# Rotary scores over 128 rows in a hybrid decoder trunk, and last projection weights loaded last

## The chip, the core and the metric

The kernel runs on one core of a Trainium2 chip. The time is the device time of one execution in microseconds (us). The core has five engines that run their own instruction queues in order: TensorE (PE, matrix products into PSUM), VectorE (DVE), ScalarE (ACT), GpSimd (POOL) and SyncE (SP, which issues the loads here).

## What is computed

Two post-norm decoder layers on 256 tokens of width 1024, each a token mixer and a gated feed-forward block. Layer 0 mixes with latent attention, which the change touches:

```python
proj = h @ w_in                                   # 1024 -> 256 + 256 + 64
c_q  = rms_norm(proj[..., :256], q_norm)
c_kv = rms_norm(proj[..., 256:512], kv_norm)
k_rope = apply_rope(proj[..., 512:], cos, sin)    # one key of 64 for all heads
q = (c_q @ w_uq)                                  # 8 heads, 128 plain + 64 rotary
q = concat(q[..., :128], apply_rope(q[..., 128:], cos, sin))
k = concat(k_plain, k_rope);  o = causal_softmax_attention(q, k, v, 192 ** -0.5)

def apply_rope(x, cos, sin):
    x1, x2 = halves(x)
    return concat(x1 * cos - x2 * sin, x2 * cos + x1 * sin)
```

Ahead of it stands `h = x * (1 + scale(c)) + shift(c)`, where scale and shift are products of a vector `c` with 1024x6144 modulation weights.

## The kernel before

Activations lie transposed: 128 features on the partitions, 256 tokens on the columns, eight such pieces `j` for the width of 1024.

The first stage (loads from line 413 on, loop from line 573 to 607) goes over `j`. For each `j` a 1 MB piece `early[j]` of modulation weights is loaded; `mod_half` multiplies each of its two halves on DVE with the spread vector and sums them into a column (`modc`); one small addition gives `gb0`; ACT makes `hin[:, j]`; PE adds five products to the accumulators of the latent query (`cqp`), the latent key (`ckp`) and the rotary key (`krp`). The projection weights come as `iraw[k]`, two `j` in each, and POOL copies their 64 rotary columns twice side by side into `krw`, so that `krp` holds the rotary key on rows 0 to 63 and again on rows 64 to 127. All loads but one are issued by SP in the order written; the positions (`posi`) are issued by ACT, and the parameters `par_sb` second of all. `rotary()` is a generator in five steps that makes the tables `sin_t` and `cos_t`: the first step runs ahead of the loop, the others at the ends of the first `j`.

The second stage (lines 1032 to 1107) makes queries, keys and values. `low_rank` is eight products of 256 columns on PE into one of three PSUM buffers (`mm`). For the rotary parts, `rope_mul` takes a result of 128 rows (two heads of 64) and makes two products on DVE, with `cos_t` and with `sin_t`; `rope_add` adds them on PE, one through the identity and one through a matrix `swap` that exchanges half blocks of 32 rows, and ACT copies the sum out. That is done once for the key (`kr`, 256 columns) and twice for the queries (`qr`, 512 columns, four heads each). Between stand the chains `rk` (scale of the latent key) and `rq` (scale of the query).

The third stage goes over the heads (class `Head`). `scores` is, for each head, a product of 128 rows (`q`, `kk`) and a product of 64 rows (`qr`, `kr`) into the same accumulator; then come softmax (DVE, ACT), `turn`, `weigh` and `rest`, and the projection in pieces. Heads 0 and 1 are scored ahead of the values (`vps`), the others in a loop.

DVE has other work throughout: modulation halves of later blocks (`mods`) and the low parts of weights that are split in two (`fill`, after ACT's `split_hi`). When the program is written, a model of the engines' times (`Clock`) places such work where it expects DVE or ACT to stand idle by 0.45 us or more; `settled` and `need` force it ahead of its readers. The order is then fixed.

Of the kernel before, what the change touches and what calls it, by code (L numbers as in the profile page):

```python
# [12 lines left out]
F32 = mybir.dt.float32  # L13
# [4 lines left out]
ALU = mybir.AluOpType  # L18
PSUM = bass.MemoryType.PSUM

P = 128
D = 1024
S = 256
NJ = D // P
H = 8
# [27 lines left out]
OFF_ROT = OFF_KN + 2  # L53
OFF_POS = OFF_ROT + 2
NPAR = OFF_POS + 2

# [132 lines left out]
def trunk_kernel(ctx: ExitStack, tc: tile.TileContext, xT, c_col, pos_row, par, mod,  # L189
# [5 lines left out]
    G = nc.gpsimd  # L195
# [3 lines left out]
    HALF = 1024  # L199
# [4 lines left out]
    one = ring("one", 1)  # L204
    raws = ring("raws", RAWS)
    wts = ring("wts", PIECES)
    act = ring("act", 2)
# [21 lines left out]
    def mod_half(u, raw, n):  # L229
        li, p0, j0, p1, j1 = units[u]  # L230
        pp, jj = ((p0, j0), (p1, j1))[n]
        w = raw[:, n * D:(n + 1) * D]
        V.scalar_tensor_tensor(w, w, 1.0, cbf, op0=ALU.mult, op1=ALU.mult,
                               accum_out=modc[:, li, pp, jj:jj + 1])
# [175 lines left out]
    par_sb = one.tile([P, NPAR], F32, name="par_sb")  # L410
    cst_sb = par_sb[:, OFF_ROT:OFF_ROT + 2]
    posci = par_sb[:, OFF_POS:OFF_POS + 2].bitcast(I32)
    z = one.tile([P, NJ, S], F32, name="z")
    Q.dma_start(cc, c_col)
    A.dma_start(posi, pos_row.to_broadcast([P, S]))
    Q.dma_start(par_sb, par)
    ce = one.tile([P, NJ], F32, name="ce")
# [3 lines left out]
    def load_mod(j, *parts):  # L421
        if j not in early:
            ring, tag = (wts, "wx") if j < PIECES else (raws, "raw")
            early[j] = ring.tile([P, 2 * HALF], F32, name="early", tag=tag)
        for p in parts:
            Q.dma_start(early[j][:, p * HALF:(p + 1) * HALF], mod[j][:, p])
        if not parts:
            Q.dma_start(early[j], mod[j])

    def load_in(k):  # L430
        iraw[k] = raws.tile([P, 2, 576], F32, name="iraw", tag="raw")
        Q.dma_start(iraw[k], w_mla_in[k])

    def load_x(a, b):
        Q.dma_start(z[:, a:b], xT[:, a:b])

    load_mod(0, 0)
    load_x(0, 2)
    load_mod(0, 1)
    load_in(0)  # L440
    load_mod(1)
# [8 lines left out]
    load_mod(6)  # L450
    load_in(3)
    load_mod(7, 0, 1)

# [48 lines left out]
    G.memset(meanr, 1.0 / 256)  # L502
    swap = one.tile([P, P], F32, name="swap")
    iv = ident.rearrange("p (a b c) -> p a b c", a=2, b=2)
    sv = swap.rearrange("p (a b c) -> p a b c", a=2, b=2)
    for b in range(2):
        G.tensor_copy(sv[:, :, b], iv[:, :, 1 - b])

# [26 lines left out]
    def rotary():  # L535

        ang = tmp.tile([P, S], F32, name="ang", tag="g")
        V.tensor_copy(posb, posi)
        V.tensor_scalar(ang, posb, cst_sb[:, 0:1], None, op0=ALU.mult)
        for dst, turn, quarter in ((sin_t, 0.0, 0.0), (cos_t, 0.25, math.pi / 2)):  # L540
            n = tmp.tile([P, S], F32, name="n", tag="t")
            V.tensor_scalar(n, ang, INV_2PI, turn, op0=ALU.mult, op1=ALU.add)
            V.tensor_scalar(n, n, MAGIC, None, op0=ALU.add)
            V.tensor_scalar(n, n, MAGIC, None, op0=ALU.subtract)
            yield
            V.scalar_tensor_tensor(dst, n, -PI2_A, ang, op0=ALU.mult, op1=ALU.add)
            V.scalar_tensor_tensor(dst, n, -PI2_B, dst, op0=ALU.mult, op1=ALU.add)
            V.scalar_tensor_tensor(dst, n, -PI2_C, dst, op0=ALU.mult, op1=ALU.add)
            if quarter:
                V.tensor_scalar(dst, dst, quarter, None, op0=ALU.add)  # L550
            V.tensor_scalar(dst, dst, PI_SAFE, -PI_SAFE, op0=ALU.min, op1=ALU.max)
            A.activation(dst, dst, AF.Sin)
            yield
        A.mul(sin_t, sin_t, cst_sb[:, 1:2])
        table(AF.Abs_reciprocal_sqrt, cos_t)
        yield

    angles = rotary()
    next(angles)
    V.tensor_copy(cb[:, 4:8], cps[1])  # L560
# [4 lines left out]
    wuqn = act.tile([P, 2, D], F32, name="wuqn", tag="v", bufs=1)  # L565
    lat = act.tile([P, 4, S], F32, name="lat", tag="hl")
    wuk = act.tile([P, 2, D], F32, name="wuk", tag="hh")
# [5 lines left out]
    for j in range(NJ):  # L573
        k = j % 2
        raw = iraw[j // 2]
        if k == 0:
            krw = tmp.tile([P, 2, 2, 64], F32, name="krw", tag="krw", bufs=1)
            G.tensor_copy(krw, raw[:, :, 512:576].unsqueeze(2).to_broadcast([P, 2, 2, 64]))
        for n in range(2):
            mod_half(j, early[j], n)  # L580
        (wts if j < PIECES else raws).done.add(early[j][:].tensor.name)
# [14 lines left out]
        for i in range(5):  # L596
            ps = cqp[:, i] if i < 2 else (ckp[:, i - 2] if i < 4 else krp)
            w = raw[:, k, i * P:(i + 1) * P] if i < 4 else krw[:, k].rearrange("p a b -> p (a b)")
            T.matmul(ps, w, hin[:, j], start=(j == 0 and i in (0, 2, 4)), stop=(j == NJ - 1 and i in (1, 3, 4)))
# [441 lines left out]

    def rope_mul(src, space):
        n = src.shape[1]
        m = space.rearrange("p (a n) s -> p a n s", a=2)
        V.tensor_mul(m[:, 0], src, cos_t.unsqueeze(1).to_broadcast([P, n, S]))
        V.tensor_mul(m[:, 1], src, sin_t.unsqueeze(1).to_broadcast([P, n, S]))
        return m

    def rope_add(dst, m):
        n = dst.shape[1]  # L1050
        ps = psy.tile([P, n, S], F32, name="swp", tag="y")
        T.matmul(ps, ident, m[:, 0], start=True, stop=False)
        T.matmul(ps, swap, m[:, 1], start=False, stop=True)
        A.copy(dst, ps)

    q = act.tile([P, H, S], F32, name="q", tag="q", bufs=1)
    qr = act.tile([P, 4, S], F32, name="qr", tag="qr", bufs=1)
    kr = one.tile([P, 1, S], F32, name="kr")
    rk = tmp.tile([P, S], F32, name="rk", tag="rstd", bufs=1)
# [10 lines left out]
    for i in range(2):  # L1070
        A.activation(sqq[i], cqp[:, i], AF.Square)
    mk = rope_mul(krp.unsqueeze(1), z[:, 0:2])
    ps0 = low_rank(wuqr, 0, 0)
    for i in range(2):
        T.matmul(rkp, meanr, sqk[i], start=(i == 0), stop=(i == 1))
    m0 = rope_mul(ps0, hin[:, 0:4])
    rsqrt(rk, rkp, eps_rms)
    for i in range(2):
        V.scalar_tensor_tensor(lat[:, 2 + i], ckp[:, i], kn2[:, i:i + 1], rk, op0=ALU.mult, op1=ALU.mult)
    ps1 = low_rank(wuqr, 0, 2)  # L1080
    rope_add(kr, mk)
    for i in range(2):
# [5 lines left out]
    V.tensor_scalar(rq, rq, -0.5 * MLA_SCALE, None, op0=ALU.mult)  # L1088
    A.copy(q[:, 0:2], low_rank(wuqn, 0, 0))
    rope_add(qr[:, 0:2], m0)  # L1090
    m1 = rope_mul(ps1, hin[:, 4:8])
    A.copy(q[:, 2:4], low_rank(wuqn, 0, 2))
    rope_add(qr[:, 2:4], m1)
    for h in range(4, H, 2):
        A.copy(q[:, h:h + 2], low_rank(wuqn, 0, h))
# [7 lines left out]
    for h in range(H):  # L1103
        po = (h % 2) * 64
        heads.append(Head(h, [(q[:, h], kk[:, h]), (qr[po:po + 64, h // 2], kr[po:po + 64, 0])],
                          v[:, :, h * P:(h + 1) * P], oh, ol))
# [266 lines left out]
```

## Time and profile before

| | us |
|---|---|
| median of 3 runs | 618.01 (617.64 to 618.23) |
| profiled execution | 617.5 |
| its span in the profile | 615.7 |
| PE busy | 590.1 (96%) |
| DVE busy | 484.5 (79%) |
| ACT busy | 365.0 (59%) |

Times in the rows are counted from the span's start. A busy PE is not PE at its peak, since ends of pipelined products are modelled. Idle time of an engine that doesn't set the end costs nothing. In a timeline, "x4" merges four instructions of one form that follow each other; the pitch from one to the next is shorter than the length of one, because starts overlap ends.

### The profile page before, as it was taken

Reading aid. Unit: us, or ns where it says so; the run is one execution under the profiler, and the core shown is the slowest. Engines: PE = TensorE matmul, PEld = TensorE weight load, DVE = VectorE, ACT = ScalarE, POOL = GpSimd, SP = SyncE. Lnnn points to the kernel's source line nnn. Section 1 sums busy time; section 2 is a strip of 40 time slices with the busy share of each in tenths; the row PEclk is TensorE's granted clock in tenths of the full one; section 3 lists DMA queues with packets and bytes.
Section 4 is the critical chain, followed back from the end, with each engine's and each line's share of the span. In section 5 each row is a group of like instructions: output and inputs, shape, how many; then the busy total and the mean of one; then the engine's idle time right before and its main releaser. Section 6 shows DMA issues by size and latency. Waiting matters only on the chain.

```text
span 615.7 us, 11313 instructions
## 1 busy us (share of the span) xinstructions
PE 590.1 (96%) x4572; PEld 563.3 (91%) x4572; DVE 484.5 (79%) x937; ACT 365.0 (59%) x660; POOL 11.5 (2%) x27
## 2 busy tenths in 40 slices
PE   3799999999999999999999999999999999999994
PEld 2577579999999999999999999999999999999992
DVE  6866989899968889889788888388997765656545
ACT  3345686777754355555778776777685545454423
POOL 2000000100000000000010000000000000000000
PEclk9999999999999999999999999999999999999998
DMA  8999868447868888889237979424789655552001
GB/s 307 417 421 421 307 226 312 176 163 278 310 233 303 298 316 309 307 311 370 102 137 274 342 283 365 175 69 147 271 314 321 246 168 181 200 193 82 2 1 69
DMA packets 22372, 149.68 MB, mean 243 GB/s; under 512 B 2608, under 2 KB 3120, under 8 KB 5040
## 3 DMA queue, kind: packets, MB, share of 16 engines
q1 hardware_dynamic: 22176, 148.83, 66.3%
q8 instruction: 36, 0.59, 0.4%
q10 hardware_dynamic: 144, 0.13, 0.1%
q14 instruction: 16, 0.13, 0.1%
HBM read 147.90 MB, written 1.05 MB: 242 GB/s over the span
## 4 chain that ended last, share of the span: by engine, by line
PE 57%; issue 31%; DMA 5%; DVE 3%; ACT 2%; POOL 1%; POOLq 0%; SPq 0%; ACTq 0%; DVEq 0%
PE abps L171 19%; PE pps L171 10%; PE ffy L171 9%; PE wops L171 7%; DMA early<-in_mod_dram 5%; PE lrp L171 3%; PE fps L171 2%; PE sps L171 2%; DVE z L171 1%; PE po L171 1%; PE vps L171 1%; ACT z L171 1%; POOL st L745 1%; PE swp L171 1%; PE tps L171 1%
## 5 line engine op out<-in xcount | busy, mean ns | idle before, releaser
L171 PE MATMUL abps<-nh,wx 128*128 128x256 f32 x1344 | 233.0, 280 | 0.0
L171 DVE TENSOR_TENSOR wx<-raw,wx 128x1024 fp32r<-128x1024 f32 x166 | 198.7, 1218 | 17.4 <-ACT wx L171 17.3
L171 PEld LDWEIGHTS abps<-nh,wx 128*128 128x128 f32 x1344 | 201.7, 188 | 0.1
L171 ACT CAST wx<-raw 128x1024 fp32r<-128x1024 f32 x166 | 170.7, 1045 | 38.2 <-PE ffy L171 18.0
L171 PE MATMUL abps<-nl,wx 128*128 128x256 f32 x672 | 179.8, 279 | 0.0
L171 PE MATMUL ffy<-gh,wx 128*128 128x256 f32 x704 | 126.0, 280 | 0.0
L171 PEld LDWEIGHTS abps<-nl,wx 128*128 128x128 f32 x672 | 123.0, 188 | 0.0
L171 PEld LDWEIGHTS ffy<-gh,wx 128*128 128x128 f32 x704 | 107.8, 188 | 0.0
L171 PE MATMUL ffy<-gl,wx 128*128 128x256 f32 x352 | 98.7, 280 | 0.0
L171 DVE SCALAR_TENSOR_TENSOR raw<-raw,cb 128x1024 f32<-128x1024 f32 x80 | 96.3, 1217 | 0.1
L171 DVE SCALAR_TENSOR_TENSOR t<-abps,par_sb,t 128x255 f32<-128x255 f32 x84 | 40.4, 481 | 41.7 <-ACT t L171 40.2
L171 ACT ACTIVATE t<-abps,par_sb 128x256 f32<-128x256 f32 x42 | 23.6, 561 | 73.9 <-PE abps L171 73.8
L171 PEld LDWEIGHTS ffy<-gl,wx 128*128 128x128 f32 x352 | 66.1, 188 | 0.0
L171 PE MATMUL wops<-oh,wx 128*128 128x256 f32 x256 | 46.3, 283 | 0.0
L171 PE MATMUL pps<-nh,wx 128*128 128x256 f32 x224 | 40.3, 285 | 0.0
L171 PEld LDWEIGHTS wops<-oh,wx 128*128 128x128 f32 x256 | 39.2, 189 | 0.1
L171 PE MATMUL wops<-ol,wx 128*128 128x256 f32 x128 | 36.0, 281 | 0.2 <-DVE ol L171 0.2
L171 PEld LDWEIGHTS pps<-nh,wx 128*128 128x128 f32 x224 | 34.0, 188 | 0.3
L171 ACT ACTIVATE z<-z,st 128x128 f32<-128x128 f32 x64 | 27.0, 449 | 10.1 <-DVE st L171 9.9
L171 PE MATMUL pps<-nl,wx 128*128 128x256 f32 x112 | 30.1, 280 | 0.0
L171 ACT ACTIVATE t<-t 128x256 f32<-128x256 f32 x44 | 18.3, 416 | 16.6 <-DVE t L171 15.4
L171 DVE TENSOR_TENSOR g<-t,abps 128x256 f32<-128x256 f32 x42 | 17.5, 417 | 13.5 <-ACT t L171 13.4
(183 smaller groups left out, 692.2 us busy)
## 6 DMA issues: line engine op xcount, KB each, us to landing
raw<-in_w_f_dram SPq DMA_DIRECT2D x66, 1024.0 KB, 5.1
raw<-in_mod_dram SPq DMA_DIRECT2D x40, 1024.0 KB, 6.5
raw<-in_w_qk_dram SPq DMA_DIRECT2D x8, 1024.0 KB, 5.9
early<-in_mod_dram SPq DMA_DIRECT2D x6, 1024.0 KB, 13.9
raw<-in_w_mla_o_dram SPq DMA_DIRECT2D x4, 1024.0 KB, 7.7
raw<-in_w_v_dram SPq DMA_DIRECT2D x4, 1024.0 KB, 7.5
raw<-in_w_moba_o_dram SPq DMA_DIRECT2D x4, 1024.0 KB, 6.7
iraw<-in_w_mla_in_dram SPq DMA_DIRECT2D x4, 576.0 KB, 13.5
```

The costliest lines, as they stand in the source:

```text
L171: b = f(*args, **kw)
L745: G.tensor_tensor(st[:, 4:6], st[:, 2:4], mhalf, op=ALU.pow)
```

## The change

The scores' rotary part is taken over 128 rows. A query's rows 0 to 63 hold its product with the cosines and rows 64 to 127 its product with the sines (`rope_q`: four products on DVE, each over 64 partitions and 512 columns, from PSUM straight to `qr`). The key's rows 0 to 63 hold the turned key and rows 64 to 127 its quarter turn, so that the product over 128 rows gives the same score. The key is made by two products over 64 partitions and one product on PE with a matrix `turn`, which POOL builds. The turns of the queries on PE, their copies on ACT and the factor of sign on `sin_t` go away. Half of `qr` lies in a longer `lat`.

In the first stage, `posi` moves to SP's queue behind the first `x`, `par_sb` goes behind the first modulation half, the last `iraw` is loaded in halves with its second half behind all modulation weights, the last modulation half is loaded and multiplied in two quarters, `krw` is copied for each `j`, and all steps of `rotary` run in the loop.

```diff
-    A.dma_start(posi, pos_row.to_broadcast([P, S]))
-    Q.dma_start(par_sb, par)
...
     load_mod(0, 0)
+    Q.dma_start(par_sb, par)
     load_x(0, 2)
     load_mod(0, 1)
+    Q.dma_start(posi, pos_row.to_broadcast([P, S]))
     load_in(0)
...
-    load_in(3)
-    load_mod(7, 0, 1)
+    load_in(3, 0)
+    load_mod(7, 0, 2, 3)
+    load_in(3, 1)
...
-    for b in range(2):
-        G.tensor_copy(sv[:, :, b], iv[:, :, 1 - b])
+    turn = one.tile([P, P], F32, name="turn")
+    for b, sign in enumerate((-1.0, 1.0, 1.0, -1.0)):
+        G.tensor_scalar(turn[:, 32 * b:32 * b + 32], ident[:, 96 - 32 * b:128 - 32 * b], sign, None, op0=ALU.mult)
+    G.tensor_tensor(turn, turn, ident, op=ALU.add)
...
-        A.mul(sin_t, sin_t, cst_sb[:, 1:2])
...
-    next(angles)
...
-    lat = act.tile([P, 4, S], F32, name="lat", tag="hl")
+    lat = act.tile([P, NJ, S], F32, name="lat", tag="hl")
...
-        if k == 0:
-            krw = tmp.tile([P, 2, 2, 64], F32, name="krw", tag="krw", bufs=1)
-            G.tensor_copy(krw, raw[:, :, 512:576].unsqueeze(2).to_broadcast([P, 2, 2, 64]))
+        krw = tmp.tile([P, 2, 64], F32, name="krw", tag="krw")
+        G.tensor_copy(krw, raw[:, k, 512:576].unsqueeze(1).to_broadcast([P, 2, 64]))
         for n in range(2):
-            mod_half(j, early[j], n)
+            if (j, n) == (NJ - 1, 1):
+                part = tmp.tile([P, 2], F32, name="part", tag="part", bufs=1)
+                for i in range(2):
+                    w = early[j][:, (2 + i) * HALF // 2:(3 + i) * HALF // 2]
+                    V.scalar_tensor_tensor(w, w, 1.0, cbf[:, i * HALF // 2:(i + 1) * HALF // 2], op0=ALU.mult,
+                                           op1=ALU.mult, accum_out=part[:, i:i + 1])
+                V.tensor_add(modc[:, 0, 0, j:j + 1], part[:, 0:1], part[:, 1:2])
+            else:
+                mod_half(j, early[j], n)
...
-    def rope_mul(src, space):
...
-    def rope_add(dst, m):
...
+    def rope_q(dst, ps):
+        dst = dst.rearrange("p (b a) s -> p b a s", a=2)
+        for a in range(2):
+            i = slice(64 * a, 64 * a + 64)
+            for o, t_ in ((0, cos_t), (64, sin_t)):
+                V.tensor_mul(dst[o:o + 64, :, a], ps[i], t_[i].unsqueeze(1).to_broadcast([64, 2, S]))
...
-    mk = rope_mul(krp.unsqueeze(1), z[:, 0:2])
+    for o, t_ in ((0, cos_t), (64, sin_t)):
+        V.tensor_mul(z[o:o + 64, 0], krp[o:o + 64], t_[o:o + 64])
     ps0 = low_rank(wuqr, 0, 0)
...
-    m0 = rope_mul(ps0, hin[:, 0:4])
+    rope_q(qr[0], ps0)
     rsqrt(rk, rkp, eps_rms)
...
     ps1 = low_rank(wuqr, 0, 2)
-    rope_add(kr, mk)
+    krt = psy.tile([P, S], F32, name="krt", tag="y")
+    T.matmul(krt, turn, z[:, 0], start=True, stop=True)
+    A.copy(kr, krt)
...
-    A.copy(q[:, 0:2], low_rank(wuqn, 0, 0))
-    rope_add(qr[:, 0:2], m0)
-    m1 = rope_mul(ps1, hin[:, 4:8])
-    A.copy(q[:, 2:4], low_rank(wuqn, 0, 2))
-    rope_add(qr[:, 2:4], m1)
-    for h in range(4, H, 2):
+    rope_q(qr[1], ps1)
+    for h in range(0, H, 2):
         A.copy(q[:, h:h + 2], low_rank(wuqn, 0, h))
...
-        heads.append(Head(h, [(q[:, h], kk[:, h]), (qr[po:po + 64, h // 2], kr[po:po + 64, 0])],
+        heads.append(Head(h, [(q[:, h], kk[:, h]), (qr[h // 4][:, h % 4], kr)],
```

## Rows read from the trace of the kernel before

**Rows 1.** the page: span; each engine's busy time, share of it, instructions
```profile
span 615.7 us, 11313 instructions
PE 590.1 (96%) x4572; PEld 563.3 (91%) x4572; DVE 484.5 (79%) x937; ACT 365.0 (59%) x660; POOL 11.5 (2%) x27
```

**Rows 2.** by stretch: length, busy time of PE, PEld, DVE, ACT, POOL; clock; DMA
```profile
8.35:26.04 17.69, 11.40 (x38) 8.81 (x39) 17.27 (x46) 7.30 (x13) 1.22 (x2) 1.00 1.02 421
...
39.20:62.52 23.32, 23.32 (x105) 19.13 (x104) 15.94 (x30) 10.74 (x20) 0.00 (x0) 1.00 0.98 407
39.20:102.98 63.78, 63.54 (x339) 49.27 (x338) 52.47 (x128) 40.50 (x98) 0.00 (x0) 1.00 0.87 337
89.40:102.98 13.58, 13.58 (x109) 13.37 (x110) 12.64 (x27) 9.25 (x19) 0.00 (x0) 1.00 0.91 338
```

**Rows 3.** waits of TensorE from 39.2 us on: total, times, longest
```profile
PE bc L171 <- POOL st L745: 1.5, 4, 0.7
```

**Rows 4.** timeline of the first stage: start, length, engine, operation, idle before it
```profile
1.63 0.42 SPq L171 DMA_DIRECT2D early<-in_mod_dram  x1
5.35 0.28 DVE L171 CAST posb<-posi 128x256 f32<-128x256 int32 x1
6.39 0.62 DVE L171 TENSOR_SCALAR n<-n 128x256 f32<-128x256 f32 x2
28.26 1.22 DVE L171 SCALAR_TENSOR_TENSOR early<-early,cb 128x1024 f32<-128x1024 f32 x1 [2.22 <-DMA early<-in_mod_dram]
29.41 1.22 DVE L171 SCALAR_TENSOR_TENSOR early<-early,cb 128x1024 f32<-128x1024 f32 x1
36.29 0.60 ACT L171 ACTIVATE hin<-z,gb 128x256 f32<-128x256 f32 x1 [2.00 <-DVE gb L171]
```

**Rows 5.** timeline of TensorE (PE) from 43 to 56 us
```profile
43.52 0.59 PE L171 MATMUL swp<-z,ident 128*128 128x256 f32 x2
43.95 0.59 PE L171 MATMUL swp<-z,swap 128*128 128x256 f32 x2
47.00 1.02 PE L171 MATMUL swp<-hin,ident 128*128 128x512 f32 x2
48.72 1.89 PE L171 MATMUL lrp<-lat,wuqn 128*128 128x256 f32 x8
55.62 7.07 PE L171 MATMUL lrp<-lat,wuk 128*128 128x256 f32 x32
```

**Rows 6.** timeline of VectorE (DVE) from 41 to 47 us
```profile
41.13 0.69 DVE L171 TENSOR_TENSOR hin<-lrp,cos_t 128x512 f32<-128x512 f32 x1 [0.91 <-PE lrp L171]
41.74 0.68 DVE L171 TENSOR_TENSOR hin<-lrp,sin_t 128x512 f32<-128x512 f32 x1
44.00 0.88 DVE L171 SCALAR_TENSOR_TENSOR lat<-ckp,kn,rk 128x256 f32<-128x256 f32 x2
45.93 0.21 DVE L171 SCALAR_TENSOR_TENSOR y<-rqp,eps_rms,y 128x2 f32<-128x2 f32 x1
46.65 0.68 DVE L171 TENSOR_TENSOR hin<-lrp,cos_t 128x512 f32<-128x512 f32 x1
```

**Rows 7.** timeline of TensorE and its weight loads (PEld), first scores
```profile
62.52 0.82 PE L171 MATMUL sps<-kk,q 128*128 128x128 f32 x4
65.82 7.13 PE L171 MATMUL vps<-wuv,lat 128*128 128x512 f32 x16
63.27 0.52 PEld L171 LDWEIGHTS sps<-kr,qr 64*128 64x128 f32 x4 [0.33 <-issue]
```

**Rows 8.** the chain that ended last, in order of time, heads 4 and 5
```profile
79.66 0.26 DVE z L171
82.64 0.26 DVE z L171
```

**Rows 9.** waits of VectorE from 39.2 to 118 us
```profile
DVE wx L171 <- ACT wx L171: 5.7, 2, 5.2
DVE z L171 <- PE wops L171: 0.8, 1, 0.8
```

More of the change, by code (lines that the diff above doesn't have):

```diff
@@ L53 @@
 OFF_ROT = OFF_KN + 2
-OFF_POS = OFF_ROT + 2
+OFF_POS = OFF_ROT + 1
 NPAR = OFF_POS + 2
@@ L410, in trunk_kernel @@
     par_sb = one.tile([P, NPAR], F32, name="par_sb")
-    cst_sb = par_sb[:, OFF_ROT:OFF_ROT + 2]
+    cst_sb = par_sb[:, OFF_ROT:OFF_ROT + 1]
     posci = par_sb[:, OFF_POS:OFF_POS + 2].bitcast(I32)
@@ L425, in load_mod, with load_in @@
         for p in parts:
-            Q.dma_start(early[j][:, p * HALF:(p + 1) * HALF], mod[j][:, p])
+            a, b = ((0, HALF), (HALF, 2 * HALF), (HALF, 3 * HALF // 2), (3 * HALF // 2, 2 * HALF))[p]
+            Q.dma_start(early[j][:, a:b], mod[j].rearrange("p a n -> p (a n)")[:, a:b])
         if not parts:
             Q.dma_start(early[j], mod[j])
-    def load_in(k):
-        iraw[k] = raws.tile([P, 2, 576], F32, name="iraw", tag="raw")
-        Q.dma_start(iraw[k], w_mla_in[k])
+    def load_in(k, *parts):
+        if k not in iraw:
+            iraw[k] = raws.tile([P, 2, 576], F32, name="iraw", tag="raw")
+        for p in parts:
+            Q.dma_start(iraw[k][:, p], w_mla_in[k][:, p])
+        if not parts:
+            Q.dma_start(iraw[k], w_mla_in[k])
     def load_x(a, b):
@@ L502, in trunk_kernel @@
     G.memset(meanr, 1.0 / 256)
-    swap = one.tile([P, P], F32, name="swap")
-    iv = ident.rearrange("p (a b c) -> p a b c", a=2, b=2)
-    sv = swap.rearrange("p (a b c) -> p a b c", a=2, b=2)
-    for b in range(2):
-        G.tensor_copy(sv[:, :, b], iv[:, :, 1 - b])
+    turn = one.tile([P, P], F32, name="turn")
+    for b, sign in enumerate((-1.0, 1.0, 1.0, -1.0)):
+        G.tensor_scalar(turn[:, 32 * b:32 * b + 32], ident[:, 96 - 32 * b:128 - 32 * b], sign, None, op0=ALU.mult)
+    G.tensor_tensor(turn, turn, ident, op=ALU.add)
     mask = one.tile([P, 384], F32, name="mask")
@@ L597, in trunk_kernel @@
             ps = cqp[:, i] if i < 2 else (ckp[:, i - 2] if i < 4 else krp)
-            w = raw[:, k, i * P:(i + 1) * P] if i < 4 else krw[:, k].rearrange("p a b -> p (a b)")
+            w = raw[:, k, i * P:(i + 1) * P] if i < 4 else krw.rearrange("p a b -> p (a b)")
             T.matmul(ps, w, hin[:, j], start=(j == 0 and i in (0, 2, 4)), stop=(j == NJ - 1 and i in (1, 3, 4)))
@@ L1040, in low_rank @@
         return ps
-    def rope_mul(src, space):
[L1043 to L1047, printed above, removed]
-    def rope_add(dst, m):
[L1050 to L1054, printed above, removed]
+    def rope_q(dst, ps):
[4 more added lines that the diff above has]
+                V.tensor_mul(dst[o:o + 64, :, a], ps[i], t_[i].unsqueeze(1).to_broadcast([64, 2, S]))
     q = act.tile([P, H, S], F32, name="q", tag="q", bufs=1)
-    qr = act.tile([P, 4, S], F32, name="qr", tag="qr", bufs=1)
-    kr = one.tile([P, 1, S], F32, name="kr")
+    qr = lat[:, 4:8], act.tile([P, 4, S], F32, name="qr", tag="qr", bufs=1)
+    kr = one.tile([P, S], F32, name="kr")
     rk = tmp.tile([P, S], F32, name="rk", tag="rstd", bufs=1)
@@ L1103, in trunk_kernel @@
     for h in range(H):
-        po = (h % 2) * 64
-        heads.append(Head(h, [(q[:, h], kk[:, h]), (qr[po:po + 64, h // 2], kr[po:po + 64, 0])],
+        heads.append(Head(h, [(q[:, h], kk[:, h]), (qr[h // 4][:, h % 4], kr)],
                           v[:, :, h * P:(h + 1) * P], oh, ol))
@@ L1315 @@
     freq = (ROPE_BASE ** (-np.arange(32) / 32)).astype(np.float32)
-    cst = np.stack([np.tile(freq, 4), np.tile(np.repeat(np.array([1.0, -1.0], np.float32), 32), 2)], axis=1)
+    cst = np.tile(freq, 4).reshape(P, 1)
     pos = np.ascontiguousarray(a["positions"].astype(np.int32).reshape(1, S))
```

## The prediction

> **What bounds the kernel now.** I read the page first: TensorE (PE) is busy for 590.1 of 615.7 us [rows 1], so time can only come from PE's work, or from the stretch in which it starves. The list of PE's waits places that stretch: after 39.2 us the largest entry is 1.5 us in four pieces [rows 3]. All other starving is ahead of 39.2 us. The timeline of that first stage shows what ends there: VectorE (DVE) multiplies each 1 MB piece of modulation weights as it lands. It runs almost unbroken to 26.04 us (17.27 of 17.69 us busy [rows 2]), waits 2.22 us for the sixth piece, and from 28.26 us goes from half to half until the last `hin` starts at 36.29 us [rows 4]. Then I read the stretch that is rewritten. From 39.2 to 62.5 us PE is busy throughout [rows 2], so work taken off PE there moves the first scores. One stretch is another matter: from about 74.5 to 89.4 us the chain runs through DVE and ScalarE, and a head's softmax follows the last at a distance of 2.98 us (79.66 to 82.64 [rows 8]), whatever PE does. From 89.4 us PE leads again. So what is won ahead of 74.5 us is kept to the end, if DVE can follow; what PE saves inside the head loop is worth nothing.
>
> **Part 1, loads and the angles.** The first modulation half is issued one place earlier, 0.47 us at most (it stood at 1.63 us, a slot of 0.42 us and a gap [rows 4]). Bytes are the same. The first stage of `rotary` (four operations from 5.35 to 7.01 us [rows 4]), which stood in idle time ahead of the loop, enters DVE's unbroken run, and each later stage moves one `j` back. DVE therefore reaches the sixth piece about 1.65 us later; the 2.22 us of idle time there [rows 4] covers it, and 0.57 us of cover is left. Without that cover it would cost 1.65 us. The last projection half now lands behind the last modulation piece, so that piece lands some 0.7 us earlier (295 KB at the 421 GB/s of [rows 2]). But DVE is the limit by then: from 28.26 to 36.29 us it runs six halves at 1.15 us (28.26 to 29.41 [rows 4]), 6.9 of the 8.0 us; the rest is small additions and some 0.3 us of waits. Those go. The last half is cut in two quarters: neither row shows a quarter, so the pair lies between 1.15 us (no fixed part) and 2.3 us (nothing saved); near the lower end, for the same form on 256 columns takes 0.44 us of 0.88 for two [rows 6], so 1.22 us, plus one small addition of 0.16. That eats what the 0.3 gave. What is left is the earlier stream: **-0.25 us**, between -0.8 (whole slot, and quarters that hide) and +0.6 (the cover too short after a later `posi`). The eight smaller copies of `krw` and the five operations that build `turn` go to GpSimd, which is busy for 11.5 us in all [rows 1]; the last copy, after the late half, has some 3 us until the last `krp`. SyncE's queue gets three more issues of 0.42 us and is ahead of the landings: nothing.
>
> **Part 2, the turns leave PE.** Of the key's two products one stays: -0.43 us (43.52 to 43.95 [rows 5]). Each of the two query turns was four passes, 47.00 to 48.72 us [rows 5]: -1.72 us each. Together **-3.87 us** of PE, all in its unbroken stretch; ScalarE loses two copies of 0.59 us that were not on the path. DVE pays: four products over 64 partitions for two over 128, twice. The trace has none over 64 partitions. Its ends are half price (0.34 us) and full price, 0.61 us from one 128x512 row to the next (41.13 to 41.74 [rows 6]); I take full price, since in this trace a vector operation's time goes with its columns. The Trainium skill (VectorE: DVE Perf Modes, the section on why `tensor_reduce` can't reduce along the partition axis) says that each of the 128 partition lanes is an independent pipeline, which speaks against this part: half the lanes idle and nothing is saved. By the page the sum below stands as it is; no row here shows it.
>
> Full price gives +1.22 us for each of the two sets. The first set ends at 43.65 instead of 42.43 us. The `rk` chain behind it ended at 44.88 and now ends near 45.95; its reader on PE, `wuk`, starts near 52, so nothing waits. Behind it come the four small `rq` operations (0.72 us, 45.93 to 46.65 [rows 6]) and then the second set, 46.65 to 49.17 us. **Here is a new wait.** The second `wuqr` result sits in one of three PSUM buffers, and the third pair of `wuqn` products needs that buffer. PE gets there at 48.30 us (first pair 0.43 earlier, then 1.73 us for each pair), so it stands until about 49.2: +0.9 us. Queued behind it are the other `wuqn` and `wuk` products and the first scores, so it counts in full. Bounds: 0 at half price, 2.05 if the planner puts a modulation half of 1.15 us ahead of the second set. Net of part 2: **-2.95 us**, between -3.87 and -1.8.
>
> **Part 3, scores over 128 rows.** A weight load ahead of or behind a 64-row group of scores starts 0.33 us after the one before it [rows 7], eight times at the 64-row groups, and the first two heads' four groups take 3.30 us, 62.52 to 65.82 [rows 7]. A 128-row group has 384 columns twice; by the pitch of 0.43 us for 256 columns twice [rows 5] that is 0.65 us, four of them 2.6 us: -0.7. The third head's pair saves 0.3 more. The other five are inside the loop of 2.98 us [rows 8] and give nothing. **-1.0 us**, between 0 (the gaps have another cause) and -1.3. The Trainium skill (TensorEngine Tiling (Array Packing), Tiling Modes, Key Properties) says that changing the tiling mode drains the array; by that the gaps go away, and the sum is this one. The same page (Overview, Theoretical Speedup) offers up to 2x for a contraction of 64 or less, which the change gives up; the kernel before doesn't take it, its 64-row groups run one after another.
>
> **Part 4, DVE's queue.** The same queue holds the modulation halves and the splits of weights, and PE needs them at the first projection. From 39.2 to 102.98 us DVE is busy for 52.5 of 63.8 us [rows 2]: 11.3 idle. The change takes 2.45 us of it for products and 3.95 us by moving PE forward, 6.4 in all. Most idle time there is latency that can't be filled; 5.7 us of it is a wait for ScalarE's half of a split [rows 9], and I take that as usable, since landed modulation pieces can be run in it. That leaves +0.7 us, which the 0.8 us of waiting for the projection at 102 us [rows 9] would absorb only if the planner's order allows. **+0.7 us**, between 0 and +4.9 (none of the 5.7 usable, the 0.8 and another 0.7 absorbed).
>
> **The sum.** -0.25 - 2.95 - 1.0 + 0.7 = -3.5 us. Against the profiled execution's 617.5 us (span 615.7): 614.0. The median of the runs is 618.0, 0.5 above it, so **614.5 us**.
>
> **Rivals.** (a) Everything is kept: no buffer wait, no backlog, the slot at the start: -0.8 - 3.87 - 1.0 = -5.7, near 612.3. For it: half-price products would do it, and the idle 5.7 us is large enough almost alone. Against: three estimates must all fall well. (b) The new wait comes at its worst (2.05) and the backlog at about 2: -0.25 - 1.8 - 1.0 + 2 = near -1, 617. For it: DVE is busy for 12.64 of the last 13.58 us before the projection [rows 2]. (c) Slower: DVE's backlog becomes the bound at the first normalisation. The planner sets the order from its own durations, and before it left 5.2 us idle at one place [rows 9], so it misjudges by that much. If the 5.7 us stays idle again and one more modulation piece (2.3 us) must be run just ahead of the column sums, the price is 4.9 + 2.3 = 7.2 against a gain of 4.2: 621. It decides from a lateness of 5.7 us at 103 us (4.2 + 1.5 of slack). Against: splits for the next block stand in the same stretch and can be put off. (d) The 128-row scores aren't shorter: 615.5, inside my range. That the change doesn't do what it says: the turned key would still need its two products; the code has one.
>
> **How the numbers follow.** A measurement of this kernel tells about 0.2% (1.2 us) from no change: faster is below 616.8. My forecast with its neighbours from 613.2 to 615.9 us, (d) in it: 0.50. (a) with what lies below 613.2: 0.21. Between 615.9 and 616.8: 0.08. (b), within 0.2%: 0.12. (c): 0.09. So faster 0.79, same 0.12, slower 0.09. Range: it leaves out (c) and the far ends of (a) and (b): 611.9 to 617.3.
>
> **What would show it.** Right: the last `hin` at 36.0 us, first `wuk` product near 52.4, first scores near 59.3, third pair of `wuqn` behind a gap of about 0.9 us, no gaps of 0.33 us in the scores, products over 64 partitions at 0.61 us. The lead should be about 4.2 us at the third head's softmax and 3.5 us in the first block. Wrong: DVE late at the projection, waits of PE on a split or on `z` between 85 and 120 us, or a lead that grows in the head loop.

## The result, and the profile after

The changed kernel is slower. Its median of 4 runs is 624.45 us (623.66 to 625.32) against 617.83 us for the kernel before, measured beside it: a ratio of 1.0107, 95% interval 1.0091 to 1.0123. The forecast was 614.5. The profiled span grows by 7.1 us, and TensorE (PE) does less than before in it (586.6 us busy for 590.1, [rows 1]):

```profile
span 622.8 us, 11309 instructions
PE 586.6 (94%) x4562; PEld 565.1 (91%) x4562; DVE 488.6 (78%) x944; ACT 362.7 (58%) x657; POOL 16.0 (3%) x34
```

So PE waits more than before. Its list of waits from 39.2 to 125 us (total, times, longest) names the place; before, nothing over 1.5 us in four pieces stood there [rows 3]:

```profile
PE wops L171 <- DVE wx L171: 7.7, 2, 6.8
```

TensorE waits at the first projection for the low part of a split weight, which VectorE (DVE) makes. The table by stretch (length; busy time of PE, PEld, DVE, ACT, POOL; granted clock, DMA share, GB/s), first the three stretches of [rows 2], then the place of the wait:

```profile
39.20:62.52 23.32, 23.06 (x113) 20.52 (x114) 17.27 (x32) 11.34 (x23) 0.00 (x0) 1.00 0.97 383
39.20:102.98 63.78, 61.43 (x354) 52.67 (x355) 52.70 (x128) 40.37 (x101) 0.00 (x0) 1.00 0.84 321
89.40:102.98 13.58, 12.76 (x105) 12.41 (x104) 11.61 (x23) 7.37 (x15) 0.00 (x0) 1.00 0.84 314
104.00:111.00 7.00, 2.85 (x25) 2.65 (x23) 6.93 (x20) 2.17 (x5) 0.00 (x0) 0.91 0.54 162
111.00:113.70 2.70, 0.01 (x1) 0.01 (x1) 2.70 (x7) 2.70 (x7) 0.00 (x0) 0.50 0.82 337
113.70:116.00 2.30, 2.30 (x11) 2.30 (x12) 2.30 (x3) 2.30 (x4) 0.00 (x0) 0.50 0.38 75
```

Two things are to be seen. VectorE is busy without a break from 104 us on while TensorE stands. And the granted clock falls to 0.50, the lower level of 1.2 GHz, while TensorE stands idle, and it is still there when the products go on: from the first product behind the wait (113.69 us) to the next block's (120.64) 47 passes take 6.95 us, where the pitch ahead of the wait (0.35 us for three) gives 5.5. VectorE's timeline shows what stands ahead of the split (start, length):

```profile
104.38 1.22 DVE L171 SCALAR_TENSOR_TENSOR raw<-raw,cb 128x1024 f32<-128x1024 f32 x1
107.25 1.22 DVE L171 SCALAR_TENSOR_TENSOR raw<-raw,cb 128x1024 f32<-128x1024 f32 x1
108.40 1.22 DVE L171 SCALAR_TENSOR_TENSOR raw<-raw,cb 128x1024 f32<-128x1024 f32 x1
109.54 0.28 DVE L171 TENSOR_TENSOR cols<-modc,par_sb 128x8 f32<-128x8 f32 x2
112.42 4.62 DVE L171 TENSOR_TENSOR wx<-raw,wx 128x1024 fp32r<-128x1024 f32 x4
```

Modulation halves, the column sums `cols` which need them, and the sums of the normalisation come first; the split that TensorE waits for starts at 112.42 us. This is the order written into the program. Below, M is a modulation half (M3 is three in a row), w0 to w7 are the splits of the first projection's weights, ol the last step of a head, GATE the gate, z a result of the projection (z2 is two in a row), COLS the column sums:

```
before   M1 M5 w0 w1 M2 M1 M3 w2 w3 M1 M1 ol M1 ol M1 ol M1 M1 ol w4 w5 ol M3 ol M3 ol ol GATE w6 z2 w7 z2 COLS z2 ...
changed  M6 w0 w1 M5 M1 w2 ol w3 ol M1 ol M1 ol M1 M1 ol M2 w4 ol w5 M2 ol ol GATE M1 z3 M1 z M2 COLS z2 w6 w7 ...
```

In the kernel before all 24 halves stand ahead of GATE and w6 right behind it. In the changed one four halves are left over behind GATE, and w6 and w7 stand behind them.

What the change did ahead of this, in four marks: the last `hin` starts at 38.80 us (36.29 before [rows 4]); the first scores start at 61.17 (62.52 [rows 7]); the third head's softmax starts at 72.17 (74.50 before); the next block's first product starts at 120.64 (113.98 before). So 2.5 us are lost in the first stage, 4.84 us are won between it and the third head's softmax, and 9.0 us are lost from there to the next block. Behind it nothing more than 0.4 us is lost.

### The profile page after: what moved, and what is told of

Its sections match the earlier page's. It is cut to its first block, busy times and chain, and to the rows that moved or that the text cites. A ratio compares the mean times of both kernels' runs of the same rounds, so it can differ in the third digit from the quotient of the medians.

```text
span 622.8 us, 11309 instructions
## 1 busy us (share of the span) xinstructions
PE 586.6 (94%) x4562; PEld 565.1 (91%) x4562; DVE 488.6 (78%) x944; ACT 362.7 (58%) x657; POOL 16.0 (3%) x34
## 3 DMA queue, kind: packets, MB, share of 16 engines
HBM read 147.90 MB, written 1.05 MB: 239 GB/s over the span
## 4 chain that ended last, share of the span: by engine, by line
PE 55%; issue 31%; DVE 8%; ACT 2%; DMA 2%; POOL 1%; SPq 0%; POOLq 0%; ACTq 0%; DVEq 0%
PE abps L171 19%; PE pps L171 10%; PE ffy L171 9%; PE wops L171 6%; PE lrp L171 3%; DVE early L171 3%; DMA early<-in_mod_dram 2%; PE fps L171 2%; DVE z L171 2%; PE sps L171 1%; ACT z L171 1%; PE vps L171 1%; DVE raw L171 1%; PE po L171 1%; DVE acc L171 1%
## 5 line engine op out<-in xcount | busy, mean ns | idle before, releaser
L171 PE MATMUL wops<-oh,wx 128*128 128x256 f32 x256 | 48.1, 289 | 7.7 <-DVE wx L171 7.7
L171 PEld LDWEIGHTS wops<-oh,wx 128*128 128x128 f32 x256 | 40.5, 194 | 8.1 <-DVE wx L171 8.1
```

The costliest lines, as they stand in the source:

```text
L171: b = f(*args, **kw)
```

## Experiments

Unless a sentence says otherwise, times are medians with the ratio to the kernel before, which took 617.5 to 617.9 us beside them.

**One half of the change each.** `first_stage_only` is the kernel before with the first stage of the changed one; `scores_only` is the changed kernel with the first stage of the kernel before.

```diff
 first_stage_only, from before          scores_only, from changed
-    A.dma_start(posi, ...)             +    A.dma_start(posi, ...)
+    Q.dma_start(posi, ...)             -    Q.dma_start(posi, ...)
+    load_in(3, 0)                      -    load_in(3, 0)
+    load_mod(7, 0, 2, 3)               -    load_mod(7, 0, 2, 3)
+    load_in(3, 1)                      -    load_in(3, 1)
...
```

> The kernel before with the first stage of the change alone (load order, positions on SP's queue, rotary steps in the loop, quarters, krw for each j); scores and turns as before. Theory 'loads': the first stage by itself costs what it cost in the changed kernel, so the last hin starts near 38.8 us instead of 36.3, the second half of modulation piece 0 lands near 10.4 us instead of 8.6, and the whole is about 620.3 us (618 + 2.5). Rival 'rows of 1372 bytes': the loads went wrong only because the parameter rows became 4 bytes shorter, which this kernel doesn't have; then the last hin is at 36 us or earlier and the time is 617.5 to 618.

Measured: 621.74 us, 1.0061 (1.0044 to 1.0078). The last `hin` starts at 36.90 us, only 0.6 us late and not near 38.8, as the first theory has it; the rival's marks aren't met either. The next block starts 2.7 us late. VectorE's order has changed here too: one modulation half is left over behind GATE, w6 stands behind it, w7 behind COLS, and TensorE waits 1.7 us for a split.

> The changed kernel with the first stage of the kernel before. Theory 'order': the splits of the last projection weights stand behind the column sums in VectorE's order whatever the first stage does, because VectorE has 2.7 us more to do and TensorE comes 4.9 us earlier; last hin at 36.3 us, third head's softmax near 69.6 us, a wait of TensorE of 6 to 9 us on a split near 102 us, whole time 621 to 623 us. Rival 'late start': the backlog comes from the late first stage; then there is no wait above 1 us and the time is about 613 us.

Measured: 622.76 us, 1.0079 (1.0060 to 1.0097). The last `hin` starts at 36.48, and the third head's softmax at 69.85, 4.65 us ahead of before. All of that and 5.9 us more is lost again by the next block's start (119.86 us); TensorE's waits from 85 to 125 us:

```profile
PE wops L171 <- DVE wx L171: 4.5, 1, 4.5
PE wops L171 <- ACT oh L171: 1.9, 1, 1.9
```

Each half is slower on its own, by 3.9 and 4.9 us. The large loss between the third head's softmax and the next block belongs to the half with the scores: 10.5 us there, 2.1 us in `first_stage_only`.

**The first stage.** `positions_on_act` is the changed kernel with `posi` back in ScalarE's queue; `positions_as_rows` loads the positions from 128 rows instead of 128 times from one; `positions_on_sp` is the kernel before with nothing but `posi` moved to SP's queue (and the first step of `rotary`, which needs it, into the loop).

```diff
 positions_on_act, from changed
+    A.dma_start(posi, pos_row.to_broadcast([P, S]))
-    Q.dma_start(posi, pos_row.to_broadcast([P, S]))
 positions_as_rows, from changed
-    Q.dma_start(posi, pos_row.to_broadcast([P, S]))
+    Q.dma_start(posi, pos_row)
-        "pos_row": pos,
+        "pos_row": np.repeat(pos, P, axis=0),
 positions_on_sp, from before
-    A.dma_start(posi, pos_row.to_broadcast([P, S]))
     load_mod(0, 1)
+    Q.dma_start(posi, pos_row.to_broadcast([P, S]))
```

> The changed kernel with one line back: the positions are issued by ACT as the first load. Theory 'positions': the 128 reads of one row of 1 KB in SP's queue put the DMA engines out of step; without them there piece 0's second half lands by 8.6 us, piece 1 by 12.6 us, the last hin starts at 35.5 to 36.3 us, and the time falls by about 2.5 us to 622. Rival 'order of the others': parameters behind the first modulation half, more transfers in the queue; then the last hin stays near 38.8 us and the time near 624.5.

Measured: 622.94 us, 1.0084 (1.0067 to 1.0100). The last `hin` is back at 36.24 us, with every other edit of the first stage in place. The wait at the projection stays (7.6 us).

> The changed kernel, the positions stored as 128 equal rows in memory and loaded row by row at the same place of SP's queue: same bytes, same packets, but no two reads of one address. Theory 'one row': 128 reads of the same 1 KB are what puts the DMA engines out of step; the second half of piece 0 lands by 8.8 us, piece 1 by 12.8 us, the last hin starts at 36.3 us, and the time is about 622. Rival 'one more transfer': any transfer of small packets at that place does it; last hin at 38 us or later, time 624.

Measured: 623.4 us, 1.0093 (1.0073 to 1.0113); last `hin` at 36.95, VectorE's start on the second modulation piece at 14.23 us (15.99 in the changed kernel, 12.78 before). That is about half way back, but `first_stage_only`, which reads the one row 128 times, stands at 14.07 us. So this run doesn't show that reading one row is a part of the cost.

> The kernel before with the positions alone moved to SP's queue, behind the second half of modulation piece 0 (the rotary steps run in the loop, as they must). Theory 'positions': piece 1 lands 1 to 4 us later than 12.6 us and the last hin starts 0.5 to 2.5 us later than 36.3; the order of splits is that of the kernel before, so the time is 618.5 to 620.5. Rival: the landings stay within 0.3 us of before and so does the last hin; 617.5 to 618.

Measured: 620.67 us, 1.0049 (1.0034 to 1.0064). VectorE's order is that of the kernel before, and no new wait over 0.5 us appears later; the loss is the move itself (the rotary step in the loop alone does no harm: `positions_on_act` has it too). Second half of the first piece, first half of the second piece, and last `hin`, in this kernel, then the two halves in the kernel before:

```profile
9.71 1.23 DVE L171 SCALAR_TENSOR_TENSOR early<-early,cb 128x1024 f32<-128x1024 f32 x1 [2.10 <-DMA early<-in_mod_dram]
15.35 1.23 DVE L171 SCALAR_TENSOR_TENSOR early<-early,cb 128x1024 f32<-128x1024 f32 x1 [2.27 <-DMA early<-in_mod_dram]
38.10 0.60 ACT L171 ACTIVATE hin<-z,gb 128x256 f32<-128x256 f32 x1 [2.00 <-DVE gb L171]
```

```profile
9.50 1.22 DVE L171 SCALAR_TENSOR_TENSOR early<-early,cb 128x1024 f32<-128x1024 f32 x1
12.78 1.22 DVE L171 SCALAR_TENSOR_TENSOR early<-early,cb 128x1024 f32<-128x1024 f32 x1
```

With one load of 128 short rows moved into SP's queue, VectorE starts on the second piece 2.6 us late and the last `hin` starts 1.8 us late. The bytes are the same as before. From 6 to 10 us the DMA engines are nearly as busy (0.97 for 1.05) but move less (stretches of this kernel, then of the kernel before):

```profile
6.00:10.00 4.00, 0.00 (x0) 0.00 (x0) 1.80 (x4) 0.00 (x0) 0.00 (x0) 1.00 0.97 258
```

```profile
6.00:10.00 4.00, 1.52 (x8) 1.12 (x6) 3.25 (x8) 0.58 (x1) 0.00 (x0) 1.00 1.05 418
```

By 16 us 4.48 MB have landed against 4.98 (4.62 in the changed kernel). At 418 GB/s those 0.5 MB are 1.2 of the 2.6 us; the rest isn't explained. Nor is the size: in the six traces with the positions in SP's queue the second piece starts at 14.07 to 15.99 us and the last `hin` at 36.90 to 38.80; in the seven with them in ScalarE's queue at 12.54 to 12.79 and 35.98 to 36.48. That the move delays the stage is shown; why it costs 0.6 us at the last `hin` in one kernel and 2.5 in another is open.

**The order at the projection.** `split_first` plans the last projection weights ahead of the last three modulation pieces. `cosine_only` is `scores_only` without the sine products (their rows hold zeros): half of the new VectorE work is left out. `turns_idle` is `scores_only` with eight idle passes of 512 columns on TensorE, which nobody reads, where the turns stood.

```diff
 split_first, from changed
-        plan_mod(3 if i < 3 else 0)
+        plan_mod((3, 3, 0, 3)[i])
 cosine_only, from scores_only
-            for o, t_ in ((0, cos_t), (64, sin_t)):
+            for o, t_ in ((0, cos_t),):
 turns_idle, from scores_only
+        if h < 4:
+            for i in range(2):
+                T.matmul(idle_ps, ident, hin[:, 0:2], start=(i == 0), stop=(i == 1))
```

> The changed kernel with the last projection weights planned ahead of the last three modulation pieces, so that VectorE splits them before the column sums. Theory 'order': the wait of 6.8 us of TensorE and the stretch at 1.2 GHz behind it go; the modulation halves then stand ahead of the column sums and cost 1 to 2 us there; 616.5 to 618.5 us. Rival 'too much work': VectorE has too much to do in any order, the wait moves to the column sums at its full size, and the time stays at 623 to 625 us.

Measured: 621.57 us, 1.0064 (1.0045 to 1.0082), between the two theories' times. The waits for the splits shrink from 7.7 to 0.8 us, and TensorE waits for the next block's input instead, since the modulation halves now stand ahead of the column sums (this kernel, then the kernel before):

```profile
114.26 4.56 PE L171 MATMUL fps<-zg,raw 128*128 128x258 f32 x12 [1.94 <-ACT zg L171]
```

```profile
113.98 2.77 PE L171 MATMUL fps<-zg,raw 128*128 128x258 f32 x12
```

The next block starts nearly as early as before the change, and the loss comes behind that: the same twelve products take 1.8 us longer, at a granted clock of 0.61 (114.26 to 118.66 us), and a wait of 1.9 us for a split of the next block follows.

> The version with the scores alone (first stage as before), leaving out the queries' sine products: their rows are zeros, so VectorE makes two products for each set, as before the change. VectorE loses 2.8 us of work against the scores-only version, TensorE is as early as there. Theory 'products': VectorE's extra products made the backlog; the wait of TensorE on a split shrinks to 1 us or less and the time is about 614 us. Theory 'arrival': VectorE was full without them, and it is TensorE's earlier arrival that it can't follow; the wait stays at 4 to 6.5 us less at most 2.8, the split stays behind the column sums, and the time is 619 to 621 us.

Measured: 623.07 us, 1.0089 (1.0072 to 1.0106); PE waits 7.7 us for splits, the longest 6.8, and VectorE's order is that of the changed kernel. With four products of 0.7 us less on VectorE nothing is won. This alone doesn't clear the products of blame, because leaving them out also changed the order (in `scores_only` two halves stand behind GATE, here four); `planner_late` below, which makes all of them, does.

> The scores-only version with eight passes of 512 columns on TensorE whose result nobody reads, in the places where the queries' turns stood (3.4 us), so that TensorE arrives about as late as before while VectorE has its 2.8 us more. Theory 'arrival': the split moves ahead of the column sums again, waits on splits sum to 2 us or less, no stretch at 1.2 GHz, 618 to 619.5 us: faster than the scores-only version with more work on TensorE. Theory 'products': the wait stays at 4 us or more and the idle passes are added: 624 to 626 us.

Measured: 619.08 us, 1.0022 (1.0011 to 1.0033): 3.7 us faster than `scores_only` with more work on the engine that bounds the kernel. The wait for a split is 1.7 us, and w6 stands ahead of the column sums. One sign failed: the granted clock still falls, to 0.57 from 112 to 116 us, behind that wait. So an earlier TensorE is what does harm; open was whether on the chip or in the model that sets the order.

**Only the model.** The order is written by `Clock`, the model of the engines' times. The next runs change one number of it, the time at which TensorE is free, in one line ahead of the first scores. No instruction is added or taken away.

```diff
 planner_early, from before             planner_late, from scores_only
+    clock.free["T"] -= 3.0             +    clock.free["T"] += 3.0
     heads[0].scores()                       heads[0].scores()
```

> The kernel before, with one number changed in the model that sets the order: where the first scores are written, TensorE is taken to be 3.0 us earlier than the model had it. No instruction is added or removed; VectorE's static order from there on becomes that of the changed kernel (the last two splits of the projection weights behind the column sums). Theory A (the order set by the planner costs the time): TensorE's wait for the splits of the last projection appears here too, of 2 to 4 us (the 6.8 us of the changed kernel less the some 4 us that TensorE is later here), the clock falls behind it, and the time is 2 to 4 us over the kernel before (620 to 622). Theory B (the work or the earlier TensorE costs it, the order does not): within 0.5 us of the kernel before, 617.4 to 618.4, no wait over 1 us for a split.

Measured: 628.12 us, 1.0171 (1.0158 to 1.0184). This is the kernel before with the same instructions (each engine's count is that of [rows 1]) in another order, and it loses 10.6 us. Its order in VectorE's queue is that of the changed kernel, step for step in the signs used above, with w6 behind the column sums, and so has the trace the wait and then the clock (waits of PE, then the table by stretch):

```profile
PE wops L171 <- DVE wx L171: 7.4, 2, 6.8
```

```profile
108.00:112.00 4.00, 1.71 (x15) 1.50 (x13) 4.00 (x10) 1.35 (x2) 0.00 (x0) 1.00 0.63 211
112.00:116.00 4.00, 0.00 (x0) 0.00 (x0) 3.93 (x15) 2.56 (x8) 0.00 (x0) 0.81 0.75 266
116.00:120.00 4.00, 3.47 (x16) 3.47 (x17) 3.88 (x4) 3.82 (x5) 0.00 (x0) 0.50 0.44 129
```

Order is the cause, as theory A has it, but the size I expected (2 to 4 us) was too small. I had thought that a TensorE which is 4 us later would find the split that much further on. VectorE is later too: its order is fixed, and it stands ahead of the first softmax until the scores come:

```profile
64.69 0.35 DVE L171 CUSTOM_DVE_ANT_0 z<-sps,mask,rq 128x128 f32<-128x128 f32 x1 [3.90 <-PE sps L171]
```

> The changed scores with the first stage of before, and TensorE taken to be 3.0 us later in the model where the first scores are written; nothing else differs from the run scores_only. VectorE's static order through the head loop and the projection becomes that of the kernel before, nearly. Theory A (order): the 4.5 us wait for a split and the fall of the clock go away or shrink below 2 us; the 4.85 us won by the first scores are kept in part, and the time is 614 to 617.5, at or under the kernel before. Theory B (VectorE's full queue is the bound in any order): TensorE waits in other places for the same sum, and the time is 619 to 622, as with scores_only or with the idle passes.

Measured: 614.42 us, 0.9952 (0.9941 to 0.9964), faster than both kernels. With the scores of the changed kernel and, through head loop and projection, the order of the kernel before (but for one modulation half, which stands a head earlier), no wait for a split is left, and the next block starts at 110.58 us (113.98 before, 119.86 in `scores_only`). The stretch from 39.2 us to GATE in this kernel, in the changed kernel and in the kernel before, then the two splits of this kernel:

```profile
39.20:97.53 58.33, 55.24 (x312) 46.58 (x311) 54.13 (x130) 36.86 (x94) 0.00 (x0) 1.00 0.90 353
```

```profile
39.20:99.11 59.91, 57.56 (x321) 48.80 (x321) 49.91 (x122) 36.73 (x96) 0.00 (x0) 1.00 0.84 320
```

```profile
39.20:100.92 61.72, 61.48 (x322) 47.21 (x321) 51.17 (x126) 38.45 (x96) 0.00 (x0) 1.00 0.86 334
```

```profile
97.60 1.22 DVE L171 TENSOR_TENSOR wx<-raw,wx 128x1024 fp32r<-128x1024 f32 x1
100.84 1.22 DVE L171 TENSOR_TENSOR wx<-raw,wx 128x1024 fp32r<-128x1024 f32 x1
```

Up to GATE VectorE stands idle for 4.2 us, against 10.0 in the changed kernel and 10.55 before. The idle time could be used; the changed order doesn't use it. The 4.0 us by which the first scores are earlier than before (58.51 us) are 3.4 at the third head's softmax and 3.4 at the next block.

Whether a VectorE with less to do would give more was asked next: `gpsimd_splits` is `planner_late` with w6 and w7 made by GpSimd, as soon as ScalarE's half is there; the functions that place splits are changed to fit.

```diff
 gpsimd_splits, from planner_late
+            if ld.aside:
+                GS.tensor_tensor(ld.wl[p], ld.raw[:, p * HALF:(p + 1) * HALF], ld.wh[p].bitcast(F32), op=ALU.subtract)
...
-        wo_loads.append(plan_weight(w_mla_o[i]))
+        wo_loads.append(plan_weight(w_mla_o[i], aside=i >= 3))
```

> As planner_late, and the low parts of the last projection weights' two halves are made on GpSimd instead of VectorE (two subtractions of 128x1024, 2.3 us of VectorE). Theory A: the order was the whole loss, so this gives nothing beyond planner_late, within 0.7 us. Theory B: VectorE's full queue is the bound, so that taking 2.3 us off it gives 1 to 2.3 us over planner_late, 613 to 618; if a GpSimd subtraction slows the VectorE work beside it, as the small copies did by 0.08 us each, part of that is lost.

Measured: 620.7 us, 1.0065 (1.0048 to 1.0081), neither theory's number. The trace kept of it has a granted clock of 0.56 from end to end, so its times can't be laid beside the others. Its order can: VectorE's is that of `planner_late` without w6 and w7, and with the next weights' first split moved up between the results. GpSimd took 2.87 and 3.17 us for the two subtractions, against VectorE's 1.22 in the rows above. That this kernel is some 6 us slower than `planner_late` is measured; where they are lost, and whether the subtractions or the changed placing lose them, is open.

Last, the whole changed kernel with the order of `planner_late`.

```diff
 changed_late, from changed
+    clock.free["T"] += 4.0
     heads[0].scores()
```

> The changed kernel, all of it, with one number changed in the model: where the first scores are written, TensorE is taken to be 4.0 us later. VectorE's order through head loop and projection is then that of planner_late (the last two splits right behind the gate, all modulation halves ahead of it). Theory A (order alone made the loss behind the third head's softmax, the first stage costs its 2.5 us at the last hin by itself): the wait for a split goes away, and the time is that of planner_late plus 1.5 to 2.8 us, 616 to 617.5, within 0.3% of the kernel before. Theory B (the late landings of the first stage take part in the loss behind the softmax too): 618 to 621, with a wait of TensorE over 2 us for a split or a modulation column.

Measured: 618.72 us, 1.0017 (1.0007 to 1.0026). The order alone gives back 5.6 of the changed kernel's 6.6 us, and the wait for a split is gone, as theory A has it; the time is in theory B's range, 4.3 us over `planner_late`. The last `hin` (38.32 us, 36.14 there) is late by 2.2 us, half of it. The rest is in ScalarE's queue, whose order the model writes too. The first split's upper half stands there behind a copy of `kk` (ScalarE's timeline of this kernel, then of `planner_late`):

```profile
59.60 0.59 ACT L171 COPY kk<-lrp 128x512 f32<-128x512 f32 x1 [1.14 <-PE lrp L171]
60.08 1.05 ACT L171 CAST wx<-raw 128x1024 fp32r<-128x1024 f32 x1
```

```profile
55.25 0.59 ACT L171 COPY kk<-lrp 128x512 f32<-128x512 f32 x1 [1.14 <-PE lrp L171]
55.73 1.05 ACT L171 CAST wx<-raw 128x1024 fp32r<-128x1024 f32 x1
```

VectorE waits for that half (this kernel, then `planner_late`):

```profile
61.16 1.23 DVE L171 TENSOR_TENSOR wx<-raw,wx 128x1024 fp32r<-128x1024 f32 x1 [2.01 <-ACT wx L171]
```

```profile
56.82 1.23 DVE L171 TENSOR_TENSOR wx<-raw,wx 128x1024 fp32r<-128x1024 f32 x1 [0.28 <-ACT wx L171]
```

In `changed_late` it is the third copy, in `planner_late` the second; the second copy itself is 2.63 us later here (57.88), the third another 1.72. The sum, 4.35 us, is the distance of everything behind it: VectorE's first softmax starts at 66.44 against 62.09, the next block at 114.94 against 110.58.

## Why the prediction was wrong, step by step

**Part 1 (-0.25 forecast, +2.5 measured).** The step that failed is the bound "+0.6 (the cover too short after a later `posi`)" and, behind it, "Bytes are the same": I counted the bytes and the slots of SP's queue and took the landings as given. One part holds: the first half starts at 6.42 us instead of 8.35, where the first stretch of [rows 2] begins. Then the pieces come late (start, length, idle time ahead of it, changed kernel):

```profile
10.40 1.23 DVE L171 SCALAR_TENSOR_TENSOR early<-early,cb 128x1024 f32<-128x1024 f32 x1 [2.75 <-DMA early<-in_mod_dram]
15.99 1.23 DVE L171 SCALAR_TENSOR_TENSOR early<-early,cb 128x1024 f32<-128x1024 f32 x1 [2.27 <-DMA early<-in_mod_dram]
36.99 0.68 DVE L171 SCALAR_TENSOR_TENSOR early<-early,cb 128x512 f32<-128x512 f32 x1
37.60 0.77 DVE L171 SCALAR_TENSOR_TENSOR early<-early,cb 128x512 f32<-128x512 f32 x1
```

From 15.99 to 38.60 us VectorE is busy for 22.06 of 22.61 us, so the delay of the second piece (3.2 us) can't be made good by the last `hin` (2.5). `positions_on_act` and `positions_on_sp` show that the positions in SP's queue do it; how large the delay is differs between kernels, and that is open. The two quarters took 1.38 us from 36.99 to their end at 38.37; I had 1.22, from start to start.

**Part 2 (-2.95 forecast, -3.86 measured).** From the last `hin` to the first scores it is 22.37 us, 26.23 before. TensorE's saving came in full: from the end of the small `rqp` products to the first scores it runs without a gap (changed kernel):

```profile
46.47 0.95 PE L171 MATMUL rqp<-meanr,sqq 128*128 128x1 f32 x8
47.28 7.15 PE L171 MATMUL lrp<-lat,wuqn 128*128 128x256 f32 x32
54.27 7.07 PE L171 MATMUL lrp<-lat,wuk 128*128 128x256 f32 x32
61.17 0.82 PE L171 MATMUL sps<-kk,q 128*128 128x128 f32 x4
```

The step that failed is "Here is a new wait": VectorE ended the second set at 52.2 us, and the third pair went on at 50.7. I had read the three buffers as taken in turn. The trace doesn't name them, but the first pair had been copied out by 49.87 us, so that a free one was there. The price of the products was right in kind: over 64 partitions nothing is saved, 0.69 to 0.73 us from one to the next, a little over the 0.61 that I took for 128. The Trainium skill (VectorE: DVE Perf Modes, on why `tensor_reduce` can't reduce along the partition axis) calls the lanes independent pipelines; the trace agrees, in that half of them idle save nothing:

```profile
49.42 0.68 DVE L171 TENSOR_TENSOR qr<-lrp,cos_t 64x512 f32<-64x512 f32 x1
50.11 0.68 DVE L171 TENSOR_TENSOR qr<-lrp,sin_t 64x512 f32<-64x512 f32 x1
51.51 0.69 DVE L171 TENSOR_TENSOR qr<-lrp,sin_t 64x512 f32<-64x512 f32 x1
```

**Part 3 (-1.0 forecast, -0.98 measured).** The first two heads' scores take 2.62 us for 3.30 [rows 7], the gaps of 0.33 us are gone, the products of the values give 0.1 and the third head 0.2 of the rest. The Trainium skill (TensorEngine Tiling (Array Packing), Tiling Modes, Key Properties) says that a change of tiling mode drains the array. The trace fits that, since the gaps went with the 64-row groups, but it doesn't show what the gaps were.

**Part 4 (+0.7 forecast, some +9 measured).** This is the step that failed and turned the sign. The sentence was "5.7 us of it is a wait for ScalarE's half of a split [rows 9], and I take that as usable, since landed modulation pieces can be run in it". As a statement on the chip it holds: `planner_late` leaves VectorE 6.35 us less idle time up to GATE than the kernel before, where I had counted on 6.4. What I didn't ask is who decides whether it is used. That wait did shrink, from 5.2 us [rows 9] to 2.0 (changed kernel, 39.2 to 118 us):

```profile
DVE wx L171 <- ACT wx L171: 2.3, 2, 2.0
```

But four halves weren't placed ahead of the gate, because the model had TensorE earlier: `planner_early`, with that alone, leaves the same four behind, and `planner_late` places all. (That the model then saw fewer idle slots in the head loop is how I read its code; no run shows it.) The bound of +4.9 that I gave priced backlog, not a change of order. The order put 24 halves and the column sums ahead of the split, which TensorE needs first, and the clock fell behind the wait: 7.7 us of waits and some 1.5 us of slow passes, 9.2 in all. A wait of PE on a split between 85 and 120 us is the sign of being wrong that the prediction named.

**The rivals.** (c) came nearest, with 0.09: VectorE's backlog at the first normalisation, 621 us, with the planner named as a reason. Its reason against it, "splits for the next block stand in the same stretch and can be put off", failed: those of the projection itself were put off. Its lateness was given in time on the chip, and what decides is the model: 3.0 us of shift in one number gives 10.6 us with not one product changed.

**The sum as measured**, to the start of the next block: +2.5 - 3.86 - 0.98 + 9.0 = +6.7 us, and 0.4 behind it make the span's 7.1. That `planner_late` came out at 614.42 us, beside the forecast's 614.5, is chance: it lacks the first stage of the change, and its gain is made up otherwise (4.0 us at the first scores, 3.4 from the third head's softmax on).

## What to carry to other kernels

Where a model of the engines' times writes a static order, an edit acts twice, on the chip and in the model; lay the two orders side by side ahead of any reading of times, and rerun with the model's clock moved by a few us to see what the order alone is worth. Here a shift of 3 us was worth 10.6 us in one kernel and 8.3 in another, and the edit of the scores, which looked like a loss of 5, was a gain of 3 once the order was held. Work that has no deadline of its own (halves for a later block) must not be placed ahead of work that the next product reads, however idle the model thinks the engine.

## What the runs showed of the hardware

With a load of 128 short rows near the head of SP's queue, VectorE started on the next 1 MB piece 1.3 to 3.2 us later in six traces, far more than the 0.3 us that its 128 KB take at the 421 GB/s of [rows 2]; in ScalarE's queue the same load cost nothing that can be seen. Whether the row being the same or the short packets do it is open. After TensorE had stood for 6.8 us, the granted clock was 0.50 at its next products, and the passes behind the wait cost some 1.5 us more. Shorter waits came out either way: after 1.75 us the clock was 0.57 in `turns_idle` (112.01 to 116 us) and 1.00 in `first_stage_only` (113.85 to 117 us). In `planner_late`, without a wait for a split, it is 1.00 throughout:

```profile
97.53:120.00 22.47, 22.21 (x164) 21.13 (x163) 19.17 (x47) 16.39 (x31) 1.62 (x1) 1.00 0.56 204
```

And a kernel with two subtractions of 128x1024 moved to GpSimd was slower although that took work from the engine that was full; why wasn't seen.
